# Tuning a one-core hybrid-layer kernel: last merged rows stay on chip, the gate's norm moves into its sigmoid and its weights, two small additions change engine, one more warming matmul

## The chip, the cores and the metric

The kernel runs on one core of one Trainium2 chip. A core has five instruction queues that run side by side: PE (matrix products and transposes), DVE (VectorE, elementwise), ACT (ScalarE, functions, copies and casts), POOL (GpSimd) and SP, which here issues every transfer between DRAM and the core's SBUF. Each queue runs its instructions in order, and an instruction that waits holds up those behind it. Results of PE land in PSUM banks (128 partitions x 512 float32). The metric is the device time of one execution in microseconds (us), the median of several.

## The reference, cut to what matters

One layer over a sequence of 1024 rows of width 1024, all in float32:

```python
h = rms_norm(x, norm_mix_g); proj = h @ w_in              # q, k, v, z_a, conv and gate inputs
y_a = (rms_norm(gla(q, k, v, gk)) * silu(z_a)) @ w_branch_a
y_c = (cb * causal_dwconv(cc * xc) * silu(z_c)) @ w_branch_c
merged = sigmoid(g_a + b_ga) * y_a + sigmoid(g_c + b_gc) * y_c
x = x + merged @ w_out
ple_gate = sigmoid(rms_norm(x, norm_ple_g) @ w_ple_gate)
x = x + ple_gate * (p @ w_ple_proj)
return rms_norm(x, norm_final_g)
# rms_norm(x, g) = x / sqrt(mean(x*x, last axis) + 1e-6) * g
```

`rms_norm(x, norm_ple_g)` multiplies row r of x by a number `rstd[r]` and column c by `norm_ple_g[c]`. A factor on a row of x is also a factor on that row of `x @ w_ple_gate`; a factor on a column of x is also a factor on that row of `w_ple_gate`.

## The kernel before

**Arithmetic.** Every large product is done by PE on pairs: a float32 operand is split into `hi` (a cast to PE's float32 format, by ACT) and `lo` (the rest, a subtraction by DVE), and one product takes three matmuls, hi·hi, lo·hi and hi·lo (`mm3`). A `Cell` takes two of the eight 128-row blocks of an activation (side A), or 256 columns of a weight matrix (side B), through all 1024 terms of the sum. It cuts both operands 2x2 and computes the product of the blocks with seven block products instead of eight (Strassen-Winograd): on side A it needs the sums S1 = a21 + a22, S2 = S1 − a11, S3 = a11 − a21 and S4 = a12 − S2, on the other side sums of the blocks b11, b12, b22, b21. The seven products accumulate in three PSUM banks, X, Y and V, of a cell; two sets of banks alternate between two cells that run as a pair (`out0` with `out1`, `out2` with `out3`, likewise `gt`). Each cell is issued in the order of products 0, 1, 2, 3, 5, 4, 6. V is used by products 1 and 5: after product 1 it is emptied through `taken("s5", ...)`, Y after product 2 through `taken("u2", ...)`, and product 5 can't start in V before.

**Order.** The program is not issued as written. Every operation is recorded (`Flow.note`; all of them are issued from the one line `o.call`, L491 in the profile), then a planner gives each a cost and a due time (`set_dues`) and simulates the five queues to fix the order of each (`put_in_order`). PE's products keep the written order; PE's small work (`nc.side`: transposes, attention) and everything on the other queues is placed where the planner expects it to be ready and due. `weave(gen, n)` has the steps of a generator follow n ticks apart beside the products. Buffers come from pools by tag, each tag with a fixed number `bufs` of buffers in rotation: a tile waits until the tile that used its buffer before has been read for the last time.

**Stages.** Warming matmuls and p·W_pe (`pe`, stored as `ped`); norm and transpose of x; then the cells v, z_a, q/k; `conv` (first product at 314.9 us) with the gates; attention (its masked tiles `aT` from 631.0 to 735.6); `yc` and `ya`, the branches' output products, and their merging; `out` (first product of `out0` at 930.4); `gt` (`gt0` at 1013.9). In detail, where the change is:

- `weights()` (L1262), in `conv`: for w = 0 (`w_out`) and w = 1 (`w_ple_gate`) and four slices kt, loads a slice `wt` of 1 MB, forms four sums of the blocks in place with DVE, and stores these to DRAM (`wtd[w][0..3]`). `bq(w)` lists the seven operands: the plain blocks from the input `wb`, the sums from `wtd`. They are later loaded as `woq` and `wgq` and split into `wo0..6hi/lo` and `wg0..6hi/lo`.
- `merge_a` (L948): when a piece of `ya` is done (transposed layout: 128 columns of the merged matrix by 512 rows; k = 0 to 7 counts the columns, i = 0, 1 the two halves of the rows), loads the gate `ga` and the convolution branch's share `mcl`, multiplies and adds (DVE), and stores the merged piece to DRAM, `md[i]`. `md[0]` feeds `out0` and `out1`, `md[1]` `out2` and `out3`. Columns k >= 4, made by `ya2` and `ya3`, which come last, are a12 and a22 of these cells (the upper and the lower 128 of their 256 rows).
- `out0` to `out3` (side A from `md`): `Cell.load(k)` loads the raw blocks (`out0raw`) that product k needs, `ring_steps` makes the sums (`out0S`) and the `hi`/`lo` rings. `make_out` (L1552) loads x's rows into tiles `x` (128x1024, called x2), adds `out`'s products to them (`onto`, for the right halves, through `taken`; `cons` for the rest), and in `finish` sums squares (ACT) per half; when a row block has both halves, x2 is stored (`x2d`), `rstd_of` makes `rg` (POOL), and `flip` scales x2 by it (ACT, 128x1024), transposes it in eights of 128x128 (`pt_g`, two PSUM buffers of four each), and DVE copies each four from PSUM, multiplied by `norm_ple_g` (`gr`), to be stored (`gd`) as operands of `gt`.
- `gt0` to `gt3` (`make_gate`): sigmoid of the product in PSUM (ACT), times `pe`, plus x2, sum of squares, final norm, output. The last row blocks go piece by piece (`piece`): for the very last, columns 512 to 1023 (a `Y`-piece of its own), 0 to 255 and 256 to 511. Each piece's sum of squares `msl` is added to the one before by POOL (`pre`), the last by POOL into `rf`, which POOL raises to −1/2; DVE and ACT then scale x, and four stores end the kernel.
- The warming matmuls (`warm`, L978) run on a tile of zeros while the first weights and rows of p are on their way.

Of the kernel before, what the change touches and what calls it, by code (L numbers as in the profile page):

```python
# [502 lines left out]
def kernel(  # L503
# [70 lines left out]
    gd = [[dram(f"gd{p}_{q}", 2, 4, P) for q in range(2)] for p in range(4)]  # L574
    wtd = [[dram(f"wtd{w}_{n}", 4, 512) for n in range(4)] for w in range(2)]

# [85 lines left out]

    def ring_steps(name, side, raw):

# [16 lines left out]
        if side == "A":  # L681
            a11, a21, a12, a22 = (r(n) for n in range(4))
            return [lambda: put(a11()), lambda: two("S1", a21, a22, ALU.add), lambda: two("S2", k("S1"), a11),
                    lambda: put(a12()), lambda: two("S3", a11, a21), lambda: two("S4", a12, k("S2"), over="S2"),
                    lambda: put(a22())]
# [9 lines left out]
    class Cell:  # L695


        def __init__(self, name, side, src, res, cons, prods=ORDER, begin=None, s1=None, u2=None, s5=None):
# [5 lines left out]
            self.steps = ring_steps(name, side, self.raw)  # L704
# [120 lines left out]

    def rstd_of(ms, name, ms2=None, tag="rstd"):
        r = sm.tile([P, 1], F32, tag=tag, name=name, bufs=4)
# [117 lines left out]

    merged = set()

    def merge_a(c, pool):  # L948
        def cons(i, j, src):
# [575 lines left out]
    def bq(w):  # L1525
        return [wb[w, 0], wtd[w][0], wtd[w][1], wb[w, 3], wtd[w][2], wb[w, 2], wtd[w][3]]

# [21 lines left out]
    with phase("late", [ph["sw"], ep]) as lp:  # L1549
        flipped = set()  # L1550

        def make_out(p, cell):  # L1552
# [3 lines left out]
            def begin():  # L1556
                for i in range(2):
                    xt.append(lp.tile([P, D], F32, tag="x", name=f"x2_{p}_{i}", bufs=4))
                    load(xt[i], x[rows(2 * p + i), :])
                    ms.append(sm.tile([P, 2], F32, tag="ms2", name=f"ms2_{p}_{i}", bufs=4))  # L1560

            def flip(i, r):
                act(xt[i], xt[i], AF.Copy, scale=r[:, 0:1])
                yield 4
                for qq in range(2):
                    pt = pso.tile([P, 4, P], F32, tag="o", name=f"pt_g{p}_{i}_{qq}", bufs=2)
                    for k in range(4):
                        kk = 4 * qq + k
                        transpose(pt[:, k, :], xt[i][:, kk * P:(kk + 1) * P])
                    g = lp.tile([P, 4, P], F32, tag="gr", name=f"gr{p}_{i}_{qq}", bufs=3)  # L1570
                    tt(g, pt, gple[:, 4 * qq:4 * qq + 4, None].to_broadcast([P, 4, P]), op=ALU.mult)
                    store(gd[p][qq][:, i], g)
                    yield 1
                flipped.add((p, i))

            def finish(i, j):
                js = slice(j * 512, (j + 1) * 512)
                act(junk[:, 0:512], xt[i][:, js], AF.Square, scale=1.0 / 32.0, accum_out=ms[i][:, j:j + 1])
                seen[i] += 1
                if seen[i] == 2:  # L1580
                    store(x2d[2 * p + i], xt[i])
                    r = rstd_of(ms[i][:, 0:1], f"rg{p}_{i}", ms[i][:, 1:2], tag="rg")
                    weave(flip(i, r), 4)

            def onto(i):
                def add(src):
                    tt(xt[i][:, 512:], src, xt[i][:, 512:], op=ALU.add)
                    return xt[i][:, 512:]
                return add

            def cons(i, j, src):
                if j == 0:
                    tt(xt[i][:, 0:512], src, xt[i][:, 0:512], op=ALU.add)
                finish(i, j)
# [7 lines left out]
        for p, c in enumerate(gts):  # L1602
            c.ready = lambda k, p=p: {(p, 0), (p, 1)} <= flipped
        with phase("sw4", lp.instead, lp) as pool:
# [4 lines left out]
        with phase("fin", [ph["sw4"]], lp) as gp:  # L1609
# [3 lines left out]
            def make_gate(p, cell):  # L1613
# [5 lines left out]
                def piece(i, cs, src, n, done):  # L1619
# [44 lines left out]
                def cons(i, j, src):  # L1664
# [6 lines left out]
                    load(t, ped[2 * p + i][:, js])  # L1671
                    act(src, src, AF.Sigmoid)
                    tt(t, src, t, op=ALU.mult)
# [82 lines left out]
```

## Time and profile before

| | |
|---|---|
| three runs | 1105.62, 1106.02, 1108.62 us; median 1106.02 |
| profiled execution | 1105.2 us, of it the span of the profile 1103.1 |
| PE busy | 1090.3 us, 99% |
| DVE busy | 864.9 us, 78% |
| ACT busy | 588.2 us, 53% |
| POOL busy | 60.9 us, 6% |
| granted clock of PE | 0.997 of full speed |

The profile shows one execution. "Busy" is the time in which an engine worked on an instruction, matmuls' ends being modelled; PE counts the products, PEld the loading of the stationary operand, which goes on beside them. `SPq` lines are transfers at the time of their issue. Times in the timeline count from the start of the span. Names such as `out0S` or `x` stand for a tile, with the buffer number left out. What can be gained is not the busy time of an engine but the time in which the last of a chain of waits ends sooner.

### The profile page before, as it was taken

Reading aid. Unit: us, or ns where it says so; the run is one execution under the profiler, and the core shown is the slowest. Engines: PE = TensorE matmul, PEld = TensorE weight load, DVE = VectorE, ACT = ScalarE, POOL = GpSimd, SP = SyncE. Lnnn points to the kernel's source line nnn. Section 1 sums busy time; section 2 is a strip of 40 time slices with the busy share of each in tenths; the row PEclk is TensorE's granted clock in tenths of the full one; section 3 lists DMA queues with packets and bytes.
Section 4 is the critical chain, followed back from the end, with each engine's and each line's share of the span. In section 5 each row is a group of like instructions: output and inputs, shape, how many; then the busy total and the mean of one; then the engine's idle time right before and its main releaser. Section 6 shows DMA issues by size and latency. Waiting matters only on the chain. (4 is left out here: it accounts for less than half of the span.)

```text
span 1103.1 us, 15242 instructions
## 1 busy us (share of the span) xinstructions
PE 1090.3 (99%) x5049; PEld 907.2 (82%) x5049; DVE 864.9 (78%) x1391; ACT 588.2 (53%) x1083; POOL 60.9 (6%) x121
## 2 busy tenths in 40 slices
PE   9999999999999999999999999999999999999996
PEld 7888888788888888888888888888888887788885
DVE  6996477889878887748649687776999879879676
ACT  6775347866543433343334376765736344558554
POOL 0000000000000000000000022220000000102022
PEclk9999999999999999999999999999999999999998
DMA  9957463358777582212212699987694878788853
GB/s 317 326 188 241 135 211 106 115 186 249 243 228 259 170 290 99 89 58 67 86 63 74 224 302 350 324 259 278 237 306 158 307 260 296 273 271 297 293 182 133
DMA packets 149118, 235.79 MB, mean 214 GB/s; under 512 B 12592, under 2 KB 66096, under 8 KB 145968
## 3 DMA queue, kind: packets, MB, share of 16 engines
q1 hardware_dynamic: 149040, 234.83, 63.5%
q8 instruction: 39, 0.64, 0.2%
q14 instruction: 39, 0.32, 0.1%
HBM read 157.19 MB, written 77.59 MB: 213 GB/s over the span
## 5 line engine op out<-in xcount | busy, mean ns | idle before, releaser
L491 ACT ACTIVATE junk<-x 128x512 bf16<-128x512 f32 (+1 forms) x33 | 20.3, 617 | 20.4 <-DVE x L491 20.0
L491 ACT ACT_TABLE_LOAD x17 | 21.8, 1283 | 3.4 <-issue 2.4
L491 POOL MEMSET t<- 128x2 f32 x8 | 0.8, 99 | 378.4 <-DVE u L491 194.8
L491 DVE TENSOR_TENSOR wt<-wt 128x512 f32<-128x512 f32 x32 | 21.4, 684 | 0.2
L491 POOL TENSOR_TENSOR or<-or,mhalf 128x1 f32<-128x1 f32 x32 | 20.4, 639 | 2.7
L491 POOL TENSOR_SCALAR rg<-ms 128x1 f32<-128x1 f32 x8 | 5.9, 736 | 265.4 <-ACT junk L491 265.4
L491 DVE SCALAR_TENSOR_TENSOR u<-t,vec,u 128x1024 f32<-128x1024 f32 x16 | 20.4, 1276 | 0.0
L491 DVE COPY_PREDICATED aT<-trim,X 128x128 f32<-128x128 int32 x32 | 9.7, 302 | 13.3 <-PE X L491 12.7
L491 ACT ACTIVATE og<-op,or 128x256 f32<-128x256 f32 x32 | 15.1, 472 | 9.0 <-POOL or L491 7.4
L491 ACT CAST aTh<-aT 128x128 fp32r<-128x128 f32 x32 | 9.5, 298 | 11.3 <-DVE aT L491 9.9
L491 POOL TENSOR_SCALAR or<-oms 128x1 f32<-128x1 f32 x32 | 8.8, 275 | 118.9 <-ACT junk L491 118.9
L491 PE MATMUL op<-vl,aTh 128*128 128x256 f32 x64 | 15.0, 316 | 0.0
L491 PE MATMUL op<-Sh,qkl 128*128 128x256 f32 x56 | 14.5, 281 | 0.0
L491 DVE TENSOR_TENSOR gr<-pt_g,vec 128x512 f32<-128x512 f32 x16 | 10.7, 685 | 4.4 <-PE pt_g L491 3.6
L491 DVE TENSOR_TENSOR oT<-op,szl 128x256 f32<-128x256 f32 x32 | 13.3, 420 | 0.8 <-DMA szl<-szd 0.6
L491 ACT ACTIVATE junk<-op 128x256 bf16<-128x256 f32 x32 | 12.3, 385 | 2.0 <-PE op L491 1.7
L491 DVE TENSOR_TENSOR Sl<-S,Sh 128x256 fp32r<-128x256 f32 x28 | 11.8, 421 | 1.4 <-ACT Sh L491 1.1
L491 PE MATMUL pe<-wpehi,pThi 128*128 128x512 f32 x32 | 12.8, 399 | 0.0
L491 PE MATMUL pe<-wpehi,pTlo 128*128 128x512 f32 x32 | 12.7, 397 | 0.0
L491 PE MATMUL pe<-wpelo,pThi 128*128 128x512 f32 x32 | 12.6, 393 | 0.0
L491 PEld LDWEIGHTS X<-vl,keh 128*128 128x128 f32 x56 | 10.5, 188 | 2.3
L491 PE MATMUL X<-qkl 128*128 128x128 f32 x64 | 12.3, 274 | 0.0
(3231 smaller groups left out, 4158.1 us busy)
## 6 DMA issues: line engine op xcount, KB each, us to landing
qkl<-qkd SPq DMA_DIRECT2D x32, 320.0 KB, 4.8
wt<-in_wb_dram SPq DMA_DIRECT2D x8, 1024.0 KB, 6.4
wtd<-wt SPq DMA_DIRECT2D x32, 256.0 KB, 3.5
vl<-vd SPq DMA_DIRECT2D x32, 256.0 KB, 4.7
vraw<-in_wb_dram SPq DMA_DIRECT2D x28, 256.0 KB, 4.2
uq<-ud SPq DMA_DIRECT2D x5, 1024.0 KB, 6.4
oq<-od SPq DMA_DIRECT2D x5, 1024.0 KB, 6.0
hq<-in_xT_dram SPq DMA_DIRECT2D x8, 512.0 KB, 8.0
```

The costliest lines, as they stand in the source:

```text
L491: o.call(*[place(a) for a in o.args], **{k: place(a) for k, a in o.kw.items()})
```

## The change

Four things, in one diff:

1. **Merged rows.** The merged pieces with i = 0 and k >= 4 (four of 128x512) are written to tiles `m4` to `m7` (tag `raw`, shared with the cells' raw blocks, 8 buffers), kept until `out0` and `out1` have used them, and stored to `md` as before. S1 of `out0` and `out1` is formed from a21 and these tiles by four 128x128 additions each (`fresh`), so that a22 is loaded only for product 6. The right halves of x2 for these two cells get tiles of their own under the tags `u2` and `s5` and are loaded at the cell's beginning as four transfers of 256 KB; left halves go to the tile `x`, 256 KB each.
2. **The gate's norm.** `flip` no longer scales x2; it transposes each half as soon as its addition is done (four transposes instead of eight at a time), ACT instead of DVE copies them from PSUM, with no factor. `rstd` becomes the column `scale` of the sigmoid (`rgate`, 8 buffers instead of 4). `norm_ple_g` goes onto the blocks of `w_ple_gate` in `weights()`: 16 ACT scalings in place (128x512), and b11, b22 and b21 so scaled are stored as well (12 stores of 256 KB), from where `bq(1)` takes them. x2 is stored in halves.
3. **The last rows' sums of squares** (`pre`, and the addition into `rf`) are added by DVE, the power stays on POOL.
4. **Ten warming matmuls** instead of nine.

```diff
-    wtd = [[dram(f"wtd{w}_{n}", 4, 512) for n in range(4)] for w in range(2)]
+    wtd = [[dram(f"wtd{w}_{n}", 4, 512) for n in range(4 + 3 * w)] for w in range(2)]
...
+            def s1():
+                if not fresh:
+                    return two("S1", a21, a22, ALU.add)
+                t = keep["S1"] = bp.tile([P, 4, P], F32, tag="T", name=f"{name}S1", bufs=4)
+                for kt in range(4):
+                    tt(t[:, kt, :], a21()[:, kt, :], fresh[kt](), op=ALU.add)
+                return put(t)
...
-                if self.raw[n] is None:
+                if self.raw[n] is None and not (self.fresh and k == 1 and n == 3):
...
-            tt(g, g, m, op=ALU.add)
+            if i == 0 and k >= 4:
+                t = late[k - 4] = bp.tile([P, 512], F32, tag="raw", name=f"m{k}", bufs=8)
+                tt(t, g, m, op=ALU.add)
+                g = t
+            else:
+                tt(g, g, m, op=ALU.add)
             store(md[i][:, :, k // 4, :, k % 4, :], g.rearrange("p (a b t) -> p a b t", a=2, b=2))
...
-    for n in range(9):
+    for n in range(10):
         mm(warm[n % 6], zero[:, 0:P], zero, start=True, stop=True)
...
                     b11, b12, b22, b21 = (t[:, n] for n in range(4))
+                    if w:
+                        for n, q in enumerate((b11, b12, b22, b21)):
+                            k = kt + 4 * (n >= 2)
+                            act(q, q, AF.Copy, scale=gple[:, k:k + 1])
+                            if n != 1:
+                                store(wtd[w][4 + (n + 1) // 2][:, kt, :], q)
                     tt(b11, b12, b11, op=ALU.subtract)
...
     def bq(w):
-        return [wb[w, 0], wtd[w][0], wtd[w][1], wb[w, 3], wtd[w][2], wb[w, 2], wtd[w][3]]
+        b11, b22, b21 = wtd[w][4:7] if w else (wb[w, 0], wb[w, 2], wb[w, 3])
+        return [b11, wtd[w][0], wtd[w][1], b21, wtd[w][2], b22, wtd[w][3]]
...
-        outs.append(Cell(f"out{p}", "A", [md[p // 2][:, p % 2, n // 2, n % 2] for n in range(4)], wres, None))
+        outs.append(Cell(f"out{p}", "A", [md[p // 2][:, p % 2, n // 2, n % 2] for n in range(4)], wres, None, fresh=[
+            lambda kt=kt, p=p: late[kt][:, (2 * p + 1) * P:(2 * p + 2) * P] for kt in range(4)] if p < 2 else ()))
...
-                    xt.append(lp.tile([P, D], F32, tag="x", name=f"x2_{p}_{i}", bufs=4))
-                    load(xt[i], x[rows(2 * p + i), :])
+                    t = lp.tile([P, D], F32, tag="x", name=f"x2_{p}_{i}", bufs=4)
+                    xt.append([t[:, 0:512], t[:, 512:]])
+                    if p < 2:
+                        xt[i][1] = bp.tile([P, 512], F32, tag=("u2", "s5")[i], name=f"x2r{p}_{i}", bufs=2)
+                        for j in (1, 0):
+                            load(xt[i][j], x[rows(2 * p + i), j * 512:(j + 1) * 512])
+                    else:
+                        load(t, x[rows(2 * p + i), :])
...
-            def flip(i, r):
-                act(xt[i], xt[i], AF.Copy, scale=r[:, 0:1])
-                yield 4
-                for qq in range(2):
-                    pt = pso.tile([P, 4, P], F32, tag="o", name=f"pt_g{p}_{i}_{qq}", bufs=2)
...
-                    tt(g, pt, gple[:, 4 * qq:4 * qq + 4, None].to_broadcast([P, 4, P]), op=ALU.mult)
-                    store(gd[p][qq][:, i], g)
-                    yield 1
-                flipped.add((p, i))
+            def flip(i, j):
+                pt = pso.tile([P, 4, P], F32, tag="o", name=f"pt_g{p}_{i}_{j}", bufs=2)
+                for k in range(4):
+                    transpose(pt[:, k, :], xt[i][j][:, k * P:(k + 1) * P])
+                g = lp.tile([P, 4, P], F32, tag="gr", name=f"gr{p}_{i}_{j}", bufs=3)
+                nc.scalar.copy(g, pt)
+                store(gd[p][j][:, i], g)
+                yield 1
+                flipped.add((p, i, j))
 
             def finish(i, j):
-                act(junk[:, 0:512], xt[i][:, js], AF.Square, scale=1.0 / 32.0, accum_out=ms[i][:, j:j + 1])
+                store(x2d[2 * p + i][:, j * 512:(j + 1) * 512], xt[i][j])
+                weave(flip(i, j), 2)
+                act(junk[:, 0:512], xt[i][j], AF.Square, scale=1.0 / 32.0, accum_out=ms[i][:, j:j + 1])
                 seen[i] += 1
                 if seen[i] == 2:
-                    store(x2d[2 * p + i], xt[i])
-                    r = rstd_of(ms[i][:, 0:1], f"rg{p}_{i}", ms[i][:, 1:2], tag="rg")
-                    weave(flip(i, r), 4)
+                    rgate[p, i] = rstd_of(ms[i][:, 0:1], f"rg{p}_{i}", ms[i][:, 1:2], tag="rg", bufs=8)
...
-                    act(src, src, AF.Sigmoid)
+                    act(src, src, AF.Sigmoid, scale=rgate[p, i][:, 0:1])
...
-                        nc.gpsimd.tensor_scalar(pre, m, EPS if n == 0 else sums[i][:, 0:1], None, op0=ALU.add)
+                        nc.vector.tensor_scalar(pre, m, EPS if n == 0 else sums[i][:, 0:1], None, op0=ALU.add)
...
-                    nc.gpsimd.tensor_scalar(r, m, sums[i][:, 0:1], None, op0=ALU.add)
+                    nc.vector.tensor_scalar(r, m, sums[i][:, 0:1], None, op0=ALU.add)
```

More of the change, by code (lines that the diff above doesn't have):

```diff
@@ L661, with ring_steps @@
             "B": ((0,), (0, 1), (2,), (3,), (2, 1), (2,), (3,))}
-    def ring_steps(name, side, raw):
+    def ring_steps(name, side, raw, fresh):
         keep = {}
@@ L682, in ring_steps @@
             a11, a21, a12, a22 = (r(n) for n in range(4))
-            return [lambda: put(a11()), lambda: two("S1", a21, a22, ALU.add), lambda: two("S2", k("S1"), a11),
+            def s1():
[5 more added lines that the diff above has]
+                return put(t)
+            return [lambda: put(a11()), s1, lambda: two("S2", k("S1"), a11),
                     lambda: put(a12()), lambda: two("S3", a11, a21), lambda: two("S4", a12, k("S2"), over="S2"),
@@ L695, with __init__ @@
     class Cell:
-        def __init__(self, name, side, src, res, cons, prods=ORDER, begin=None, s1=None, u2=None, s5=None):
+        def __init__(self, name, side, src, res, cons, prods=ORDER, begin=None, s1=None, u2=None, s5=None, fresh=()):
             self.name, self.side, self.src, self.res, self.cons = name, side, src, res, cons
@@ L703, in __init__ @@
             self.raw, self.ring = [None] * 4, {}
-            self.steps = ring_steps(name, side, self.raw)
+            self.steps, self.fresh = ring_steps(name, side, self.raw, fresh), fresh
         def load(self, k):
             for n in NEED[self.side][k]:
-                if self.raw[n] is None:
+                if self.raw[n] is None and not (self.fresh and k == 1 and n == 3):
                     self.raw[n] = bp.tile([P, 4, P], F32, tag="raw", name=f"{self.name}raw{n}", bufs=8)
@@ L824, in ev, with rstd_of @@
         return ep.tile([P, 512], F32, tag="ev", name=name, bufs=3)
-    def rstd_of(ms, name, ms2=None, tag="rstd"):
-        r = sm.tile([P, 1], F32, tag=tag, name=name, bufs=4)
+    def rstd_of(ms, name, ms2=None, tag="rstd", bufs=4):
+        r = sm.tile([P, 1], F32, tag=tag, name=name, bufs=bufs)
         if ms2 is None:
@@ L944, in merge_c @@
         return cons
-    merged = set()
+    merged, late = set(), {}
     def merge_a(c, pool):
@@ L1549 @@
     with phase("late", [ph["sw"], ep]) as lp:
-        flipped = set()
+        flipped, rgate = set(), {}
         def make_out(p, cell):
@@ L1576, in finish @@
+            def flip(i, j):
[7 more added lines that the diff above has]
+                flipped.add((p, i, j))
             def finish(i, j):
-                js = slice(j * 512, (j + 1) * 512)
@@ L1585, in onto @@
             def onto(i):
                 def add(src):
-                    tt(xt[i][:, 512:], src, xt[i][:, 512:], op=ALU.add)
-                    return xt[i][:, 512:]
+                    tt(xt[i][1], src, xt[i][1], op=ALU.add)
+                    return xt[i][1]
                 return add
@@ L1592, in cons @@
                 if j == 0:
-                    tt(xt[i][:, 0:512], src, xt[i][:, 0:512], op=ALU.add)
+                    tt(xt[i][0], src, xt[i][0], op=ALU.add)
                 finish(i, j)
@@ L1602 @@
         for p, c in enumerate(gts):
-            c.ready = lambda k, p=p: {(p, 0), (p, 1)} <= flipped
+            c.ready = lambda k, p=p: {(p, i, j) for i in range(2) for j in range(2)} <= flipped
         with phase("sw4", lp.instead, lp) as pool:
@@ L1671, in cons @@
                     load(t, ped[2 * p + i][:, js])
-                    act(src, src, AF.Sigmoid)
+                    act(src, src, AF.Sigmoid, scale=rgate[p, i][:, 0:1])
                     tt(t, src, t, op=ALU.mult)
```

4 lines of the change are left out of this document (removed).

## The prediction

> **What bounds the kernel now.** I read the page first, then the windows stage by stage, then the timeline round every stretch in which PE was not full, and last the chain of work that ended last.
>
> ```profile
> span 1103.1 us, 15242 instructions
> PE 1090.3 (99%) x5049; PEld 907.2 (82%) x5049; DVE 864.9 (78%) x1391; ACT 588.2 (53%) x1083; POOL 60.9 (6%) x121
> ```
>
> PE is the bound from end to end. A change can only shorten PE's work, close a hole in it, or shorten what follows its last matmul. The windows (columns: PE, PEld, DVE, ACT, POOL busy with counts, granted clock, DMA share, GB/s) show where holes are near the change:
>
> ```profile
> 300.00:400.00 100.00, 100.00 (x443) 82.82 (x442) 83.87 (x137) 40.52 (x71) 0.40 (x4) 1.00 0.68 233
> 400.00:500.00 100.00, 100.00 (x443) 82.83 (x442) 66.22 (x99) 36.82 (x65) 0.20 (x2) 1.00 0.32 108
> 920.00:940.00 20.00, 19.27 (x84) 15.35 (x83) 18.37 (x26) 8.81 (x12) 0.00 (x0) 1.00 0.93 327
> 940.00:960.00 20.00, 19.36 (x84) 15.13 (x83) 16.96 (x28) 8.84 (x18) 0.92 (x2) 1.00 0.76 281
> ```
>
> PE has none in 300 to 500, where the weights are prepared, and two in 920 to 960, where `ya` ends and `out0`, `out1` begin. The timeline there (start, duration, and in brackets the idle time with its releaser):
>
> ```profile
> 935.32 0.69 DVE L491 TENSOR_TENSOR out0S<-out0raw,out0raw 128x512 f32<-128x512 f32 x1
> 935.65 0.39 PE L491 MATMUL out1X<-wo0hi,out1lo 128*128 128x512 f32 x1
> 936.10 0.62 ACT L491 CAST out0hi<-out0S 128x512 fp32r<-128x512 f32 x1 [0.76 <-DVE out0S L491]
> 936.77 0.50 PE L491 MATMUL out0V<-wo1hi,out0hi 128*128 128x512 f32 x1 [0.73 <-ACT out0hi L491]
> ...
> 945.66 2.07 SPq L491 DMA_DIRECT2D x<-in_x_dram  x4
> 953.54 0.68 DVE L491 TENSOR_TENSOR x<-out0V,x 128x512 f32<-128x512 f32 x1
> 953.56 0.39 PE L491 MATMUL out1X<-wo3hi,out1lo 128*128 128x512 f32 x1
> 954.37 0.47 PE L491 MATMUL out0V<-wo5hi,out0hi 128*128 128x512 f32 x1 [0.42 <-DVE x L491]
> ```
>
> A 128x512 matmul starts 0.227 us after the one before. The 144 intervals from 930.44 (first of `out0X`) to 965.81 (first of product 6) take 35.37 us against 32.65 at that pace: 2.72 lost. The first hole, 1.55 with the slow starts after it, is `out0S`: merged rows went to DRAM and back before the addition. The second, at 954.37 and 957.56, 1.12, is the bank of `out0V`/`out1V`, freed late because x2's rows, ordered at 945.66, came late.
>
> The tail and the transposes:
>
> ```profile
> 966.71 0.39 PE L491 MATMUL out0Y<-wo6lo,out0hi 128*128 128x512 f32 x1
> 966.94 1.03 PE L491 MATMUL pt_g<-ident,x 128*128 128x128 f32 x8
> 968.28 0.40 PE L491 MATMUL out0Y<-wo6lo,out0hi 128*128 128x512 f32 x1
> ...
> 1017.29 0.39 PE L491 MATMUL gt1X<-wg0hi,gt1hi 128*128 128x512 f32 x1
> 1017.57 0.63 PE L491 MATMUL pt_g<-ident,x 128*128 128x128 f32 x4
> 1018.50 0.39 PE L491 MATMUL gt1X<-wg0hi,gt1hi 128*128 128x512 f32 x1
> ...
> 1096.32 0.80 POOL L491 TENSOR_SCALAR pre<-msl,pre 128x1 f32<-128x1 f32 x1 [0.28 <-ACT junk L491]
> 1097.20 0.68 POOL L491 TENSOR_SCALAR rf<-msl,pre 128x1 f32<-128x1 f32 x1
> 1097.97 0.57 POOL L491 TENSOR_TENSOR rf<-rf,mhalf 128x1 f32<-128x1 f32 x1
> 1098.57 0.49 DVE L491 SCALAR_TENSOR_TENSOR x<-x,rf,gfin 128x256 f32<-128x256 f32 x1 [0.83 <-POOL rf L491]
> ```
>
> PE's last matmul starts at 1093.01; what follows is these steps, then DVE to 1099.32, the stores and the end at 1103.1.
>
> **The change part by part.** The order of PE is the same up to `out`'s last products, one warming matmul apart.
>
> *Merged rows kept.* `out0S` and `out1S` each become four 128x128 DVE additions on tiles already on chip instead of one 128x512 (0.69). No 128x128 addition is in the trace; between the 128x1 to 128x4 operations (0.16) and 128x256 (0.42) I take 0.2, so 0.8 for 0.69: nothing for DVE. The four kept tiles are merged by 923.76 (the last store, at 923.81, waits for it), where before this store (5.6 median to landing) and a load behind it (issued 929.56, 4.7) came first. What is left is `a21`'s load, now ahead of those stores in SP's queue, so issued by about 925 to 926 and landed by 931, and DVE's queue, which is through with `wo4lo` at about 930. Eight additions end at 931.7; cast 0.62 and `lo` 0.69 put `out0hi` and `out0lo` at about 933; `out0V` is due at 935.88, 2.8 us later. Hole 1: **−1.55** (0 if `a21` came 4 us later; no lower). Two loads of 256 KB move from product 1 to product 6.
>
> *x2's right half early.* Four 256 KB loads go to SP's queue behind `ya`'s last gate loads, at about 927 to 930, once the `s5` buffers are free (DVE reads the last at 929.49), some 16 us before 945.66. With 7.6 us from issue to landing, the additions are ready by 941 to 947; they were needed at 952.9 to 957. Hole 2: **−1.12**. The queue behind them carries `mcl` for `ya3` and the third `out0raw`; 1 MB at 327 GB/s is 3.2 us, less 1.6 for the two loads taken out. `out0raw`'s third piece is used at 942.17, loaded at 931.7 with 4.7 to landing: 5.8 us of cover. 0. If both covers failed, at most +1.6.
>
> *Transposes in fours.* A group of eight costs 968.28 − 966.71 − 3×0.227 = 0.89 of PE; a group of four 1018.50 − 1017.29 − 3×0.227 = 0.53 and, at 1019.87, 0.45: 0.49. Before, the 64 transposes stand as 7 eights and 2 fours, after as 1 eight and 14 fours: 14×0.49 + 0.89 − 7×0.89 − 2×0.49 = **+0.54** (0 to 0.8). Each now waits for a DVE addition, with its PSUM buffer (two) emptied by ACT (a 128x512 PSUM copy is 0.58) instead of DVE (0.68, 16 times, now off DVE). In ACT's queue the copy stands behind casts that wait for operand rings that PE frees; by the order of ACT the fourth and sixth group have 0 to 0.25 us to spare. Before, these groups cost PE 0.35 of waiting in all, so I take **+0.15** (−0.3 to +3).
>
> *Gate norm on sigmoid and weights.* Eight ACT scalings 128x1024 (1.145) go, off PE's way. 16 ACT scalings 128x512 (about 0.62, 9.9 in all) and 12 stores of 256 KB come into 300 to 500, where ACT is 37 to 41% busy and DMA 0.32 to 0.68: hidden. The in-place DVE subtraction on b11 waits for that tile's store: landing is 2.4/3.5/4.3 us (min, median, max) for the 32 stores of `wtd` from 334 to 416, and the order leaves about 5.3 between store and subtraction. Behind it on DVE stand splits that PE consumes, some 2.7 us ahead. 0; a store that lands after 8.0, with 12 more of them about, would cost what is over: at worst +1. The sigmoid with a column as scale may take 0.1 more (128x512 with `rf` 0.72, with a constant 0.62); the last one, done at 1093.69, is read by DVE at 1094.87: 0.
>
> *POOL additions to DVE.* In the tail 0.80 + 0.68 of POOL become two small DVE operations (128x4: 0.16). Adding up DVE's queue from 1092.73 at 0.60 per 512, 0.33 per 256 and 0.1 to 0.16 per small one ends it at 1098.65, not 1099.32: −0.65. But POOL's power takes 0.56 to 3.33 us in its eight cases, the longest at 1050.91 beside back-to-back DVE tensor_tensors, and DVE is now without its 0.83 gap. I take **−0.4** (−1.3 to +0.5).
> The Trainium skill, "SBUF — State Buffer", section "SBUF: two separate sides", says that DVE and GpSimd share a port pair under an exclusive lock that a DVE operation with two SBUF inputs holds; the row of 3.33 agrees. By it alone the power would wait for a product of 0.74 and the tail would gain nothing: 0.4 more than my sum.
>
> *Tenth warming matmul.* Nine run from 1.44; the third real one waits for `pTlo` until 5.75 in any case. The tenth (0.24 at the speed reached, 0.43 at the early one) pushes the first two real ones into that wait of 0.15, or 0.1 past it. 0 (−0.2 to +0.3).
> The Trainium skill, "TensorE: Matmul & The Clock Gate", section "What's actually happening", puts the gate's window at about 3.4 us; here the spacing falls from 0.427 to 0.235 at 4.6, 3.2 after the first. By it the tenth buys no clock.
>
> Sum: −1.55 − 1.12 + 0.54 + 0.15 − 0.4, −0.05 for rounding in the hole = **−2.4**. The profiled execution took 1105.2 (span 1103.1, 2.1 round it), 0.8 under the median 1106.02; it becomes 1102.8, and the median **1103.6**. 0.3% of the time, 3.3 us, is about what a measurement can tell from no change; it lies at 1102.7 and 1109.3.
>
> **The rivals.** (B) *More gain.* The fours fill gaps that the eights left (0 instead of +0.54, none waits), and the power isn't blocked, so the tail gains 1.0: −2.7 − 1.0 = −3.7, 1102.3. For it: 16×0.68 leave a DVE that is 82% busy there. Against: three measured groups. (C) *The gain stays away.* Hole 1 remains because `a21`'s load lands after 934: it shares 0.93 of busy DMA with the x2 loads. −2.4 + 1.55 = −0.85, 1105.2. Against: 4 us of cover. (D) *Slower.* ACT's copies, queued behind casts that PE must release, hold PSUM, and each of 15 groups then stops PE. From 0.16 per group the gain is gone; from 0.38 (5.7 in all) the kernel is over 1109.3. For it: two buffers and 53% of ACT; against: before, DVE, far fuller, emptied them for 0.35.
>
> **How the numbers follow.** My forecast 0.42 (its own range 1102.6 to 1104.6), B 0.25, C 0.17, D 0.16 with most of it beyond 1109. Faster by 0.3% is B and the lowest part of the forecast: 0.35. Slower is D: 0.16. The rest 0.49. The range goes from B's end with the tail at −1.3 (1101.8) to C with one hole more (1107.4).
>
> **What would show it.** In the trace after: `out0S` by 932 and no PE idle at `out0V`; x2's right halves ordered near 928; 15 groups `pt_g` at 0.49; POOL's last power before 1097.9; no PE hole in 300 to 500. I am wrong if groups `pt_g` show idle time by ACT `gr`, if `out0hi` is again PE's releaser, or if DVE waits on `wtd` stores so that PE stops.

## The result, and the profile after

| | before | changed |
|---|---|---|
| median of the runs measured together (7 and 7) | 1108.28 us (1105.62 to 1110.15) | 1102.77 us (1102.23 to 1104.64) |
| profiled execution | 1105.2 us, span 1103.1 | 1102.23 us, span 1100.4 |

The ratio is 0.9961, 95% interval 0.9946 to 0.9975: faster by about 0.4%. The forecast was 1103.6. Three figures for the gain don't agree, and this became the question of the study: the profiled executions differ by 3.0 us, the lowest runs by 3.4, the medians by 5.5. The runs of the kernel before are spread over 4.5 us, those of the changed kernel over 2.4.

From the head of the page of the changed kernel:

```profile
span 1100.4 us, 15273 instructions
PE 1089.4 (99%) x5050; PEld 908.3 (83%) x5050; DVE 855.8 (78%) x1386; ACT 598.2 (54%) x1107; POOL 56.0 (5%) x116
```

The windows of the changed kernel for the stages shown of before (columns as there):

```profile
300.00:400.00 100.00, 100.00 (x443) 82.78 (x442) 82.71 (x135) 45.02 (x79) 0.40 (x4) 1.00 0.73 243
400.00:500.00 100.00, 100.00 (x443) 82.81 (x442) 67.26 (x100) 41.30 (x73) 0.20 (x2) 1.00 0.39 129
920.00:940.00 20.00, 20.00 (x90) 16.57 (x89) 20.00 (x36) 10.61 (x15) 0.00 (x0) 1.00 1.04 365
940.00:960.00 20.00, 20.00 (x94) 16.57 (x93) 18.02 (x29) 8.02 (x16) 0.00 (x0) 1.00 0.78 266
```

ACT's 16 scalings are there (45.0 and 41.3 instead of 40.5 and 36.8 busy) and PE stays full. PE is full in 920 to 960 as well, where 1.4 us had been idle. The timeline round the two former holes and the first transposes, changed kernel:

```profile
927.71 2.85 SPq L491 DMA_DIRECT2D x2r<-in_x_dram  x4
930.30 0.89 DVE L491 TENSOR_TENSOR out0S<-out0raw,m 128x128 f32<-128x128 f32 x4
931.80 0.62 ACT L491 CAST out0hi<-out0S 128x512 fp32r<-128x512 f32 x1
935.86 0.39 PE L491 MATMUL out1X<-wo0hi,out1lo 128*128 128x512 f32 x1
936.09 0.39 PE L491 MATMUL out0V<-wo1hi,out0hi 128*128 128x512 f32 x1
...
940.94 0.68 DVE L491 TENSOR_TENSOR x2r<-out0V,x2r 128x512 f32<-128x512 f32 x1
...
952.18 0.39 PE L491 MATMUL out1X<-wo3hi,out1lo 128*128 128x512 f32 x1
952.41 0.39 PE L491 MATMUL out0V<-wo5hi,out0hi 128*128 128x512 f32 x1
...
957.62 0.39 PE L491 MATMUL out1V<-wo5hi,out1lo 128*128 128x512 f32 x1
957.85 0.60 PE L491 MATMUL pt_g<-ident,x 128*128 128x128 f32 x4
958.21 0.47 PE L491 MATMUL out0Y<-wo4hi,out0hi 128*128 128x512 f32 x1
...
958.75 0.39 PE L491 MATMUL out0Y<-wo4hi,out0lo 128*128 128x512 f32 x1
```

Four 128x128 additions took 0.89, the cast began at 931.80, and `out0V` follows `out1X` at the usual 0.23. The addition that empties `out0V` starts at 940.94, and product 5 starts in it at 952.41, again 0.23 after `out1X`. From 957.62 to 958.75 there are three intervals and one group of four: 1.13 − 3×0.227 = 0.45.

From the first matmul of `out0X` to the last of all, PE needed 162.57 us before (930.44 to 1093.01) and needs 160.10 (930.65 to 1090.75): −2.47. Behind the last matmul's start, DVE's last operation ended 6.31 later before and ends 5.79 later now: −0.52. Up to `out0X` the changed kernel is 0.21 late, and from DVE's end to the end of the span it takes 0.17 longer. Together that is −2.6, the difference of the spans; the remaining 0.3 to 0.4 us between the profiled executions lie outside the span. None of it explains 5.5.

One hole is new. Timeline of the changed kernel:

```profile
1083.71 1.57 POOL L491 TENSOR_SCALAR rf<-ms 128x1 f32<-128x1 f32 x1 [1.94 <-ACT junk L491]
...
1085.96 1.28 DVE L491 SCALAR_TENSOR_TENSOR x<-x,rf,gfin 128x1024 f32<-128x1024 f32 x1 [0.77 <-POOL rf L491]
1087.16 0.68 DVE L491 TENSOR_TENSOR gt3s<-gt3Y,gt3s 128x512 f32<-128x512 f32 x1
1087.90 0.39 PE L491 MATMUL gt3Y<-wg6hi,gt3hi 128*128 128x256 f32 x1
```

POOL needed 1.57 us for one addition on one column (0.30 to 2.60 for the others of this kind in the profile), DVE waited for `rf` behind it, what stood behind on DVE was late, and so was `gt3Y`, by 0.2. In the kernel before the same addition took 1.57 too (at 1085.97), and `gt3Y` followed 0.24 after the matmul ahead of it. PE now comes there 2.44 earlier and this chain only 2.26.

### The profile page after: what moved, and what is told of

It is laid out like the page before. It is cut to its first block, busy times and chain, and to the rows that moved or that the text cites. A ratio compares the mean times of both kernels' runs of the same rounds, so it can differ in the third digit from the quotient of the medians.

```text
span 1100.4 us, 15273 instructions
## 1 busy us (share of the span) xinstructions
PE 1089.4 (99%) x5050; PEld 908.3 (83%) x5050; DVE 855.8 (78%) x1386; ACT 598.2 (54%) x1107; POOL 56.0 (5%) x116
## 4 chain that ended last, share of the span: by engine, by line
PE 96%; ACT 2%; DVE 2%; issue 0%; POOL 0%; DVEq 0%; ACTq 0%
PE vacc L491 7%; PE op L491 3%; PE pe L491 2%; PE X L491 2%; PE ga2Y L491 1%; PE ga3Y L491 1%; PE ga1Y L491 1%; PE ga0Y L491 1%; PE out1Y L491 1%; PE gc1Y L491 1%; PE out0Y L491 1%; PE gc0Y L491 1%; PE out3Y L491 1%; PE out2Y L491 1%; PE za0Y L491 1%; PE xc3Y L491 1%
## 5 line engine op out<-in xcount | busy, mean ns | idle before, releaser
L491 ACT ACTIVATE junk<-x 128x512 bf16<-128x512 f32 (+1 forms) x29 | 17.8, 615 | 12.0 <-DVE x L491 11.5
L491 PE MATMUL op<-ident,og 128*128 128x128 f32 x64 | 12.3, 273 | 0.0
```

The source lines that it names most:

```text
L491: o.call(*[place(a) for a in o.args], **{k: place(a) for k, a in o.kw.items()})
```

## The experiments

The parts are named as in the change: kept merged rows, x2's right halves early, the gate's norm, additions on DVE, the tenth warming matmul. Two theories at first. Theory 1 is the prediction's sum. Its rivals put the gap between 3 and 5.5 us on one part each: the warming matmul, or the gate's norm.

### One part alone, and the warming matmul

Kernel before with ten warming matmuls, and changed kernel with nine (the same edit turned back):

```diff
-    for n in range(9):
+    for n in range(10):
```

> The kernel before with ten warming matmuls, nothing else. The seven runs of the kernel before reach from 1105.62 to 1110.15 us, those of the changed kernel only from 1102.23 to 1104.64, so the median fell by 5.5 us and the lowest by 3.4; the two profiled executions differ by 2.7 in span. Theory 1, that of the prediction: the tenth warming matmul is hidden by the wait for pTlo and worth 0 (-0.2 to +0.3); the median stays at that of the kernel before, its spread too. Rival: PE's clock turns at another moment in each execution (at 4.6 us in the profile of before, past 5.9 in that of after); with nine, some executions still are at the low clock when PE stops for pTlo and stay there for longer, and these are the runs at 1108 to 1110. Then with ten the runs lie together near 1105.5, and the median falls by 1 to 2.5 us (ratio 0.998 to 0.999).

> The changed kernel with nine warming matmuls, as before. Theory 1 (the tenth is worth 0): 1102.8, with the same spread as the changed kernel, since its spread has another cause. Rival (the tenth keeps PE busy until the clock turns): runs spread over 4 us again, from 1102.2 to 1107, median 1 to 2.5 us above the changed kernel's.

Measured: 1106.82 us (1105.42 to 1112.0, 12 runs) beside 1107.23 for the kernel before (1105.07 to 1111.61, 29 runs), ratio 1.0 (0.9985 to 1.0016); and 1102.83 (1102.28 to 1103.57, 6 runs). No effect of the tenth warming matmul can be seen, and the spread comes and goes without it: the kernel before keeps it with ten, the changed kernel lacks it with nine. The rival is out.

The gate's norm alone, and the additions alone (only the lines of the diff that belong to them):

```diff
+                            act(q, q, AF.Copy, scale=gple[:, k:k + 1])
...
-                act(xt[i], xt[i], AF.Copy, scale=r[:, 0:1])
...
+                nc.scalar.copy(g, pt)
...
-                    act(src, src, AF.Sigmoid)
+                    act(src, src, AF.Sigmoid, scale=rgate[p, i][:, 0:1])
```

> The kernel before with the second part alone: norm on the sigmoid's scale and on the gate's weights, transposes in fours, scaled blocks stored; merged rows, x2's loads, POOL's additions and nine warming matmuls as before. Prediction: +0.54 for 15 groups instead of 9 and +0.15 for waits, so +0.7, PE without a hole in 300 to 500. Second theory, from the trace of after, where 14 groups of four cost 0.44 each and none waits: -0.1 on PE; but with x2 late again the transposes may wait, +0.3. Rival that this part brings what the median shows beyond the profile: -2 or more.

```diff
-                        nc.gpsimd.tensor_scalar(pre, m, EPS if n == 0 else sums[i][:, 0:1], None, op0=ALU.add)
+                        nc.vector.tensor_scalar(pre, m, EPS if n == 0 else sums[i][:, 0:1], None, op0=ALU.add)
...
-                    nc.gpsimd.tensor_scalar(r, m, sums[i][:, 0:1], None, op0=ALU.add)
+                    nc.vector.tensor_scalar(r, m, sums[i][:, 0:1], None, op0=ALU.add)
```

> The kernel before with the third part alone: pre and the addition into rf on DVE. Prediction: -0.4 behind the last matmul (-1.3 to +0.5), nothing elsewhere. By the trace of after, in which the last matmul starts 5.79 before DVE's end instead of 6.31: -0.5. Rival: POOL's power is held up by DVE's products (1.48 for two in the trace of after, against 0.57 to 0.67 for one before) and what is gained by the additions is lost there: 0.

Measured: the gate's norm alone 1104.40 (1104.02 to 1105.19, 12 runs), ratio 0.9973 (0.9963 to 0.9984); the additions alone 1106.86 (1105.33 to 1108.82), ratio 0.9997 (0.9985 to 1.001). In the profile of the additions alone DVE ends 5.69 after the last matmul's start instead of 6.31, so the part does what it says; in runs spread over 3.5 us it can't be seen.

The gate's norm, which I had at +0.7, gains: 1 us by the lowest runs (1105.07 to 1104.02) and 2.8 by the median, because its runs lie together. Most of its second hole is gone as well, though x2 still came late (ordered at 945.85). Timeline of the kernel with the gate's norm alone:

```profile
953.76 0.39 PE L491 MATMUL out1X<-wo3hi,out1lo 128*128 128x512 f32 x1
954.05 0.63 PE L491 MATMUL pt_g<-ident,x 128*128 128x128 f32 x4
954.73 0.47 PE L491 MATMUL out0V<-wo5hi,out0hi 128*128 128x512 f32 x1
```

`out0V` starts 0.97 after `out1X`, before 0.81: it waits for the same addition on DVE, but a group of transposes stands in the wait, which has to be done at some time anyway. Beyond the price of the group, about 0.4 us of the hole's 1.12 are left. Groups no longer have to wait for both halves of a row block and its `rstd`, so there are some to put there.

### One part undone

```diff
-            lambda kt=kt, p=p: late[kt][:, (2 * p + 1) * P:(2 * p + 2) * P] for kt in range(4)] if p < 2 else ()))
+            lambda kt=kt, p=p: late[kt][:, (2 * p + 1) * P:(2 * p + 2) * P] for kt in range(4)] if False else ()))
...
-            if i == 0 and k >= 4:
+            if False:
```

> The changed kernel with S1 of out0 and out1 from blocks loaded back, as before (no kept tiles); x2's right halves, gate norm, additions on DVE and ten warming matmuls as changed. Theory (prediction): hole 1 is back, +1.55 (1.1 to 1.6) at out0V, released by ACT out0hi behind DVE out0S; 1104.3 us. Rival: with four loads of x2 ahead of it in SP's queue the load comes later still, +2.5 or more; other rival: DVE's room and another order close the hole anyway, below +0.3. The spread of the runs stays that of the changed kernel (1102.2 to 1104.6).

```diff
-                    if p < 2:
+                    if False:
                         xt[i][1] = bp.tile([P, 512], F32, tag=("u2", "s5")[i], name=f"x2r{p}_{i}", bufs=2)
```

> The changed kernel with x2's rows loaded whole into the late tile, as before; kept merged rows and all else as changed. Prediction: hole 2 is back, +1.12. Second theory, from the gate part alone, where transposes stand at 954.05 and 957.57 just in the places where PE had waited: the wait is filled with transposes that are due anyway, so below +0.3.

> The changed kernel with POOL's additions (pre, rf) back. Its runs lie close together, so this part shows. Prediction for the part: -0.4 (-1.3 to +0.5), so 1103.2; by the profile of the part alone (the end 9.5 after the last matmul's start, not 10.1): 1103.4. Rival (POOL's power is held up and gives the gain back): 1102.8.

(the last with the additions' four lines turned back.) Measured: without the kept rows 1104.79 (1104.15 to 1106.83, 12 runs), 2.0 above the changed kernel's 1102.77; with x2 loaded whole 1102.13 (1101.69 to 1102.54, 5 runs); with POOL's additions 1102.50 (1102.07 to 1103.29, 5 runs), where 1103.2 was expected. The changed kernel was not run again beside these, so a difference of about half a microsecond from it can't be told from none. In the profiles PE needs 160.13 from `out0X` to its last matmul with x2 loaded whole and 160.10 in the changed kernel.

The kept rows are thus the part with the largest effect in the changed kernel, and the early x2 gains nothing beside the other parts. But the reason is not the one expected, that transposes fill its hole. Timeline with x2 loaded whole:

```profile
943.26 2.08 SPq L491 DMA_DIRECT2D x<-in_x_dram  x4
...
950.62 0.68 DVE L491 TENSOR_TENSOR x<-out0V,x 128x512 f32<-128x512 f32 x1
952.76 0.39 PE L491 MATMUL out1X<-wo3hi,out1lo 128*128 128x512 f32 x1
952.99 0.40 PE L491 MATMUL out0V<-wo5hi,out0hi 128*128 128x512 f32 x1
...
954.59 0.60 PE L491 MATMUL pt_g<-ident,x 128*128 128x128 f32 x4
```

No group of transposes stands ahead of product 5. x2 was ordered 2.4 us earlier than in the kernel before (945.66), the addition that empties `out0V` starts at 950.62 instead of 953.54, and product 5 follows at the usual 0.23: the hole does not arise. With the gate's norm alone x2 was ordered as late as before, so it is probably the kept rows, which end the first hole and move loads in SP's queue, that bring it forward; the kept rows alone were not run.

Of the additions 0.4 us are seen in the profile (DVE ends 6.18 after the last matmul's start with POOL, 5.79 without) and none in the medians, whose ranges overlap.

The execution that was profiled without the kept rows was that kernel's slowest run, 1106.83, and it shows what a hole can cost. Its timeline, and a window of PE's clock:

```profile
936.98 0.69 DVE L491 TENSOR_TENSOR out0S<-out0raw,out0raw 128x512 f32<-128x512 f32 x1 [0.57 <-DMA out0raw<-md]
938.43 0.50 PE L491 MATMUL out0V<-wo1hi,out0hi 128*128 128x512 f32 x1 [2.38 <-ACT out0hi L491]
...
939.96 0.63 PE L491 MATMUL out0V<-wo1hi,out0lo 128*128 128x512 f32 x1
```

```profile
938.00:940.00 2.00, 1.57 (x6) 1.01 (x7) 1.59 (x3) 0.58 (x2) 0.00 (x0) 0.98 1.09 371
940.00:943.00 3.00, 3.00 (x9) 2.35 (x8) 3.00 (x6) 2.85 (x6) 0.00 (x0) 0.50 0.22 67
943.00:946.00 3.00, 3.00 (x14) 2.46 (x13) 3.00 (x6) 1.00 (x2) 0.00 (x0) 0.94 0.00 0
```

The load of `out0raw` was late, PE stood still for 2.4 us, and 1.5 us after it had started again the granted clock fell to 0.50: eight matmuls from 939.96 to 943.37 at 0.43 instead of 0.23, 1.6 us more. Counted against the pace of 0.227, that stretch loses 4.5 us; in the profile of before it loses 1.6. In the kernel before, the hole at the same place is 1.12 from start to start, and the clock stays at 1.00. The other 11 runs of this kernel lie at 1104.15 to 1105.88 and none is profiled, so their hole isn't known.

The Trainium skill, "TensorE: Matmul & The Clock Gate", section "What's actually happening", has the clock go back after at least one idle window of about 3.4 us. The time at the low clock agrees, 3.41; the idle time needed doesn't: here the clock fell after 2.4.

### What spreads the runs of the kernel before

Over the four measurements on record the kernel before ran 87 times: median 1106.48, 28 runs at 1108 or above, 44 below 1106.5. Of the seven beside the changed kernel four were at 1108 or above. So 1108.28, and with it the 5.5, is partly the draw of these seven; from 1106.48 the changed kernel's median is 3.7 lower.

Which wait of before is it that the gate's norm takes away? ACT's queue at 1018, and PE at 1023, kernel before:

```profile
1018.74 1.05 ACT L491 CAST wg6hi<-wgq 128x1024 fp32r<-128x1024 f32 x1 [1.06 <-DMA wgq<-wtd]
...
1020.88 1.04 ACT L491 CAST wg6hi<-wgq 128x1024 fp32r<-128x1024 f32 x1
1021.83 1.15 ACT L491 ACTIVATE x<-x,rg 128x1024 f32<-128x1024 f32 x1
```

```profile
1023.51 0.39 PE L491 MATMUL gt1V<-wg1hi,gt1lo 128*128 128x512 f32 x1
1023.74 1.03 PE L491 MATMUL pt_g<-ident,x 128*128 128x128 f32 x8
```

ACT waits for the load of `wgq`, although product 6 is far off; behind the cast stands the scaling of x2, done at 1022.98, and PE takes it up for the transposes at 1023.74. That is 0.8 us to spare behind a transfer. Three theories were set against each other: the chain through POOL's power and ACT's scaling (P), the gate weights' load (W), DVE's wait for `gr` buffers (G).

```diff
-                act(xt[i], xt[i], AF.Copy, scale=r[:, 0:1])
-                yield 4
...
-                    act(src, src, AF.Sigmoid)
+                    act(src, src, AF.Sigmoid, scale=rgate[p, i][:, 0:1])
```

> The kernel before with one thing of the gate part: rstd goes to the sigmoid, and x2 is transposed without the scaling by ACT. DVE's copies with norm_ple_g, three gr buffers, transposes four steps after the addition and the gate weights from the input stay. It asks what makes the runs of before spread from 1105.1 to 1111.6 (29 runs, median 1107.2) when those with the whole gate part lie within 1104.0 to 1105.2. Theory P (the chain sum of squares, POOL's power, ACT's scaling, transposes, with 0.3 to 1.2 us to spare before PE needs it, is stretched in some executions): the spread is gone, median 1104.5 to 1105.5. Theory W (the gate weights' loads come just in time: ACT waits 0.9 and 1.1 for wgq in the profile of before, and everything behind on ACT with it): spread stays unless these loads move. Theory G (DVE waits for gd stores to give back a gr buffer, 0.8 in before, 2.0 in the kernel with the third part alone): spread stays.

```diff
+            if name == "wg":
+                ts = []
+                for c in range(2):
+                    ts.append(pool.tile([P, 2, 512], F32, tag="f", name=f"{name}q{n}_{c}", bufs=5))
+                    load(ts[c], src[n][:, 2 * c:2 * c + 2, :])
+                return ts
```

(In the first, `norm_ple_g` stays in DVE's copy; in the second, `resident` takes the two halves.)

> The kernel before, the gate weights' raw tiles loaded as halves of 512 KB into five half buffers instead of two whole ones of 1 MB, so that a load can go out one half earlier; the rest as before. Theory W: no wait of ACT for wgq is left, the spread shrinks to about 1 us, the median falls to 1105.2. Theories P and G: the spread stays, median within 0.5 of before.

Measured: rstd in the sigmoid 1105.00 (1104.71 to 1105.31, 11 runs); half tiles 1105.43 (1104.87 to 1106.93, 11 runs); the kernel before beside them 1106.37 (1105.36 to 1111.2, 29 runs). Either one takes most of the spread away (0.6 and 2.1 us are left of 5.8), so neither P nor W alone is right. G is out: both kept three `gr` buffers, and DVE still waited 1.3 us in all for `gd` in the second. P and W are two ends of one chain: with half tiles ACT no longer waits for `wgq`; without the scaling it waits 1.4 us, and nothing that PE needs soon stands behind. So the next pair disturbed that chain on purpose, with one more transfer of 1 MB ahead of the load (`extra` is a spare block in DRAM and a block of the weights):

```diff
             for o in order:
+                if o.name.startswith("wgq6<-"):
+                    o.call(place(self.extra[0]), place(self.extra[1]))
                 o.call(*[place(a) for a in o.args], **{k: place(a) for k, a in o.kw.items()})
```

> The kernel before with one more transfer, 1 MB from DRAM to DRAM, issued just ahead of the load of wgq for product 6; the order of every other queue is the same, instruction by instruction. At 327 GB/s it takes 3.2 us, so the load lands some 3 us later. Theory C (what spreads the runs of before is a chain: the gate weights' load arrives with nothing to spare, ACT waits for it in order, the scaling of x2 stands behind it in ACT's queue, and PE has 0.5 to 0.8 us before it needs the transposes): in the profile ACT waits about 4 us for wgq instead of 1.1, PE stands 2 to 2.5 us at pt_g near 1023, and after such a hole the matmuls run at 0.427 for some 3 us, +1.4 more; time 1108 to 1111 in nearly all executions. Rival (the load is not needed before product 6, so ACT's wait is idle time; the spread comes from elsewhere): 1106 to 1107.5, spread as before, no hole at pt_g beyond 0.5.

> The same extra transfer in the kernel before with rstd moved to the sigmoid. Here no scaling of x2 stands behind the cast of wg6 on ACT, only casts for gt's operands. Theory C: the transposes are long done, PE's order goes on; at most 1 us is lost where gt0's and gt1's casts come late; 1105 to 1106, runs within 1 us. Rival (any wait of ACT there reaches PE, with or without the scaling): as much later as in the kernel before, 1108 or more.

Measured: in the kernel before 1108.17 (1106.78 to 1110.33, 12 runs), 1.9 above the kernel before measured beside it (1106.23, 22 runs), ratio 1.0018 (1.0009 to 1.0027); with rstd in the sigmoid 1105.11 (1104.50 to 1105.98, 11 runs), 0.1 above the same kernel without the transfer. The timeline of the kernel before with the extra transfer (it has two more lines of code, so L493):

```profile
1021.09 1.05 ACT L493 CAST wg6hi<-wgq 128x1024 fp32r<-128x1024 f32 x1 [3.10 <-DMA wgq<-wtd]
...
1024.03 1.15 ACT L493 ACTIVATE x<-x,rg 128x1024 f32<-128x1024 f32 x1
```

```profile
1023.97 0.39 PE L493 MATMUL gt1V<-wg1hi,gt1lo 128*128 128x512 f32 x1
1025.23 0.66 PE L493 MATMUL pt_g<-ident,x 128*128 128x128 f32 x4 [0.87 <-ACT x L493]
1026.04 0.65 PE L493 MATMUL pt_g<-ident,x 128*128 128x128 f32 x4 [0.15 <-DVE gr L493]
```

ACT waited 3.1 (I had expected 4), the scaling began 2.2 later, and PE stood 0.87 for it (expected 2 to 2.5) and kept its clock. From `out0X` to its last matmul PE needs 2.2 us longer than in the kernel before. Some 1.45 of this lies at these transposes; about 0.5 at a group at 1018.03 and 0.2 near 1007 come before this wait of ACT, so the transfer cost something in other ways too. The 12 runs form two groups, five at 1106.78 to 1107.19 and seven at 1108.14 to 1110.33, where nearly all were expected at 1108 or above; the profile shows the fastest of the lower group. The same transfer with the scaling gone, rstd in the sigmoid:

```profile
1020.38 2.00 ACT L493 CAST wg6hi<-wgq 128x1024 fp32r<-128x1024 f32 x2 [2.21 <-DMA wgq<-wtd]
```

ACT waits 2.2, and PE shows no wait at all there. The chain is shown: a transfer that makes this load come 2 us later costs the kernel before about 2 us, most of it at the transposes behind the scaling, and 0.1 where the scaling isn't behind the load on ACT. What is not shown is one of the high runs of the kernel before itself: its profiled execution, and those with ten warming matmuls and with the additions alone, were each among the lowest of their kernel. That the runs at 1108 to 1111 are this chain is inferred from the distributions. Whether the clock falls in them is open: of 80 runs of the kernel before with a granted clock on record it is 0.996 or lower in 10 of the 24 at 1108 or above, and in 4 of the 41 below 1106.5. In the kernel without the kept rows the profiled run, in which the clock fell, has 0.996, the other 11 have 0.997 or 0.998. A fall can thus be part of some high runs; most show the clock of the low ones.

### x2 loaded whole, and more additions on DVE

x2 loaded whole, and the other rows' sums of squares in the last norm added by DVE too:

```diff
-                        r = rstd_of(ms[i][:, 0:1], f"rf{p}_{i}", ms[i][:, 1:2])
+                        r = sm.tile([P, 1], F32, tag="rstd", name=f"rf{p}_{i}", bufs=4)
+                        nc.vector.tensor_scalar(r, ms[i][:, 0:1], ms[i][:, 1:2], EPS, op0=ALU.add, op1=ALU.add)
+                        nc.gpsimd.tensor_tensor(r, r, mhalf, op=ALU.pow)
```

> The changed kernel with x2 loaded whole, as in the run that showed 1102.13, and the sum of squares of the other rows of the last norm (rf<-ms) added by DVE too. In the trace of after POOL needed 1.57 us for that addition at 1083.71, DVE waited 0.77 for rf behind it, and gt3Y started 0.2 late. Theory: this hole of 0.2 goes and no other comes, 1101.9. Rival: DVE's addition waits for ACT's sum in DVE's queue and holds up what is behind it, 1102.3 or more.

Measured: 1101.90 (1101.19 to 1102.09, 5 runs), ratio to the kernel before 0.9957 (0.9945 to 0.9969). PE has no hole at `gt3Y` any more, and DVE ends 5.42 after the last matmul's start. It is 0.9 below the changed kernel's median and 0.2 below the kernel with x2 loaded whole, whose runs overlap with its own; neither was run beside it. In the profiles it needs 159.82 from `out0X` to the last matmul instead of 160.10.

## Why the prediction was right, and where it was wrong

The forecast, 1103.6 with 1102.6 to 1104.6 as its own range, holds the measured 1102.77; the forecast of −2.4 compares with −3.0 between the profiled executions (−2.6 in span) and −3.25 from the median it was counted from. That the sum came so near is in part luck: it put some 0.8 too much on the transposes and their waits, and what it left out (the hole at `gt3Y` 0.2, a start 0.21 later, 0.17 more at the end) took most of that back. The ends of its outer range don't come out of its own terms: B with the tail at −1.3 gives 1102.0, not 1101.8, and C with the second hole open as well 1106.3, not 1107.4. Step by step:

- *Merged rows kept, −1.55.* Right, and by the mechanism given: `out0S` at 930.30, `out0hi` at 932.4, no wait at `out0V`. Taking the part out again costs 2.0, more than the hole of before. In the one profile of it, its slowest run, three of the x2 loads go out ahead of the store and the load that `out0S` waits for, the hole is 2.76 from start to start, and the clock falls.
- *x2's right half early, −1.12.* Right in the changed kernel, by the mechanism given: ordered from 927.71, `out0V` emptied from 940.94, product 5 without a wait at 952.41. Wrong as a price: it took for granted that without this part the hole would stand beside the other three. With x2 loaded whole it doesn't arise, because x2 is then ordered at 943.26, and the kernel is no slower. The gate's norm alone leaves about 0.4 of the 1.12, since transposes, no longer bound to `rstd`, move into the wait. So the part is worth nothing beside the others; what it is worth alone was not run.
- *Transposes in fours, +0.54, and +0.15 of waits.* Wrong in size. 14 groups cost 0.44 to 0.46 each, where I had 0.49 as the mean of two; one of these two, 0.53, had a late start of its own in it. An eight costs 0.89, so two fours are an eight: 7.10 in all against 7.22, and no group waits. The 0.35 of waiting read for the groups of before was not PE's: 0.29 of it is PEld idle ahead of the group at 1017.57, where PE lost about 0.1. Rival D, in which each of them does, had no ground here: the copies on ACT didn't stand behind the casts for long.
- *Gate norm on sigmoid and weights, 0 on PE in 300 to 500.* Right. DVE waits 1.28 for a `wtd` store at 416.38, but so it did before (1.31 at 416.32), and PE is full in both.
- *Additions, −0.4.* −0.52 in the profile of the changed kernel and −0.62 alone; the medians can't tell. POOL's power wasn't held up beyond 0.93 in the tail: the two take 0.93 and 0.58. The sentence by the rule of the Trainium skill, "SBUF — State Buffer", section "SBUF: two separate sides" (the tail gains nothing), didn't come true in the profiles; POOL's 1.57 us at 1083.71 beside DVE's 128x1024 product agrees with the rule itself.
- *Tenth warming matmul, 0.* No effect in the runs. In the profile the third product came 0.7 later than before, at 6.46, so the wait until 5.75 did not cover it; 0.14 were left at 30 us.
- *Not in the prediction:* the new hole of 0.2 at `gt3Y`, and the spread. I had summed one execution. The kernel before pays for a chain with less than 1 us to spare behind a transfer in some of its executions only, and the profiled one wasn't among them; in the medians the gate's norm is worth 1.4 (rstd alone, 1106.37 to 1105.00) to 2.8 (the whole part, 1107.23 to 1104.40), where my sum had it at +0.7. Rival B's 1102.3 came closer than the forecast. Of its two grounds one held, the fours cost nothing extra and none waits; its tail gain of 1.0 wasn't there (0.52).

## What to carry to other kernels

A profile prices the waits that its execution had. Look also for chains in which an engine waits in order for a transfer that is needed much later, with work behind it that PE needs soon; count the time to spare, and compare the spread of the runs, since such a chain shows there and not in the trace. A hole of PE can be closed by removing its cause, be filled with other work, or fail to arise because another edit brings the late load forward, so edits that each close it don't add up. And a median of seven runs of a kernel whose runs spread is itself a draw.

## What the runs showed of the hardware

The clock: without the kept rows PE's granted clock fell to 0.50 for 3.4 us after a hole of 2.4 us, 1.5 us after the work had gone on (one case); holes of 1.12 to 1.39 from start to start (0.9 to 1.2 beyond the usual pace; the longest in the kernel with ten warming matmuls) left it at 1.00. At the start, with nine or ten warming matmuls from 1.44 on, the spacing went from 0.427 to 0.23 at 4.59 in some profiles and as late as 7.55 in another (POOL's additions back). The last product of `pe` starts between 29.5 and 30.6 us in the 14 profiles, each of another kernel, and not in the order of these turns: with the additions alone the turn came at 4.93 and that product at 30.39. The start thus differs by more than half a microsecond from profile to profile, which hides smaller effects.

Transposes: four 128x128 transposes between 128x512 matmuls cost PE 0.44 to 0.46 in the changed kernel, eight 0.89. POOL's addition of one column took from 0.30 to 2.04 us in the same kernel (`rg` before: 0.30, 0.44, 2.04 as least, median and most).
